# Six of seventeen gate tiles moved from the units of branch B to the following units of branch A

## The chip, the cores and the metric

The kernel runs on one core of one Trainium2 chip. It is one launch that takes all inputs from device memory and writes ten outputs there. The metric is the device time of an execution in microseconds; three runs of the kernel before gave a median of 2362.17 us (2360.77 to 2366.52).

## The reference

One layer of a streaming encoder, for a prompt of 2048 tokens and 8 running streams of 16 new tokens each, that have a cache of 512 positions. Model width is 1024.

```python
h = rms_norm(x, norm_g) * (1.0 + scale) + shift          # adaLN
qa, ka, va, za, qb, kb, vb, zb, ga, gb = split(h @ w_in)  # 4 x 512, 4 x 512, 2 x 1024
oa = diff_attention(rope(qa), rope(ka), va, lam)          # 4 heads, two softmaxes each, 64-token chunk mask
ob = stick_breaking_attention(qb, kb, vb)                 # 8 heads, strictly causal
ya = (rms_norm(oa, subln_g) * (1.0 - lam_init) * silu(za)) @ w_branch_a
yb = (ob * silu(zb)) @ w_branch_b
x = x + gate * ((sigmoid(ga) * ya + sigmoid(gb) * yb) @ w_out)
y = rms_norm(x, final_g)
```

The rotated keys and the values of both branches are outputs too. The part that matters here is the projection of the merge gates `ga` and `gb`: the last 2048 columns of `h @ w_in`. They are needed only in the last stage of the kernel, so it is open when they are computed.

## The kernel before

Tokens lie in 17 tiles of 128 rows: the prompt's tiles 0 to 15, and a tile called `NT` (16) with the 8 x 16 sample tokens. Single-precision products are made of three half-precision ones (high by high, high by low, low by high), so every projection of a tile with inner dimension 1024 is 3 x 8 = 24 matmuls of up to 512 columns.

*Stages.* A first stage makes the normed and modulated `h`, splits it in two half-precision parts and stores it transposed (`hT_d`). The middle stage, which takes most of the time, runs through 8 units. The last stage merges the branches, does the attention of the sample tokens over their caches, and makes the final norm.

*Units.* Unit `u` has head group `u // 2` of branch `u % 2`: even units are branch A (differential attention, one head), odd units branch B (stick breaking, two heads). A unit passes over its tiles in the order NT, 0, 1, ... 15. For each tile it projects query, key, value and the silu gate (one `project`, 12 pieces of 2 matmuls), transposes query and key on TensorE (`transpose_qk`, beside piece 5 of the next projection), and for the prompt's tiles computes scores against all earlier tiles (`scores`), turns them to weights, and multiplies by the values two tiles later (`PV_LAG`, `pv`). A prompt tile `t` costs about (t + 1) blocks, so tiles at the start of a unit are small and tiles at its end large.

*Branch A* evacuates scores on DVE (L546), takes exponentials on ACT (L119 from L580), combines both softmaxes on DVE (L591), splits on ACT and DVE, and transposes the weights by DMA (L568). *Branch B* takes two sigmoids of the scores on ACT (L119 from L550 and L551), scans on DVE (L604), multiplies on GpSimd (L610), splits on ACT and DVE (L560, L561) and transposes by DMA. Scores use three PSUM banks, projections two, value products two; one bank, `t`, serves the gates, the transposes of query and key and some sums.

*Gates.* The 2048 gate columns are cut in four pieces of 512 by the table `GATES` (L58): only odd units have one, as wide as the table says. In an odd unit every tile has 12 pieces more (`gate_piece`, L485 to L496): 24 matmuls of the same `h` tile with the gate weights `wg` (L492), an eviction on ACT with a scale (L495), and a store to `g_d` (L496). The 17 gate tiles of each of the four odd units make 68.

*Order.* `line` (L858 to L868) holds the pieces of all projections and gates of all units in order. For each attention tile `take` (L876) cuts off as many pieces as the weight of the tile says (`duration`, L886, with a lead of 5 tiles), and `interleave` (L91) mixes them with the tile's scores and value products. So small tiles get few pieces and large tiles many, and the projections of the first tiles of a unit stand beside the largest tiles of the unit before it. The recording layer then has a scheduler that may move an instruction within an engine's queue where dependences allow.

*Weights.* `prepare_unit` (L305) returns 9 pieces for a unit of branch A and 18 for one of branch B: loads of 4 buffers of projection weights with their sums of squares on ACT (L270), the scale, the split of each in two halves; and the same for 4 buffers of gate weights. It is called when the unit before starts (L1220) and its pieces are spread over some ten tiles by `W_READY` (L1224). Buffers come from the list `free` and go back when a unit starts: those of the unit before it (L843). In tiles with no such piece left, `spare` (L1228) puts loads and sums of squares for the last stage.

The lines below are the functions that the diff touches.

Of the kernel before, what the change touches and what calls it, by code (L numbers as in the profile page):

```python
# [20 lines left out]
AF = mybir.ActivationFunctionType  # L21
# [6 lines left out]
KT = D // P  # L28
# [4 lines left out]
NT = SEQ // P  # L33
# [10 lines left out]
W_READY = 9  # L44
# [11 lines left out]
SAMPLE_TIME = 0.3  # L56

GATES = [(u // 2 * 512, u % 2 * 512) for u in range(8)]  # L58

C_ROPE = 0  # L60
C_ID = C_ROPE + 17 * 96
# [48 lines left out]
def layer_kernel(ctx: ExitStack, tc: tile.TileContext, a: dict):  # L110
    nc = tc.nc
    V, S, G, T = nc.vector, nc.scalar, nc.gpsimd, nc.tensor
# [61 lines left out]
    def buffers_of_4k(name, n):  # L174
        pool = ctx.enter_context(tc.tile_pool(name=name, bufs=1, side="right", reuse_waits="tile"))
        return [pool.tile([P, 1024], F32, name=f"{name}{i}") for i in range(n)]


    free = buffers_of_4k("wa", 8)
# [5 lines left out]
    def bank(tag, dt=F32):  # L185
        return ps.tile([P, 512 if dt == F32 else 1024], dt, tag=tag, name=f"ps_{tag}", bufs=BANKS[tag])
# [19 lines left out]
    def total(col, n=1):  # L206

        p = bank("t")
        T.matmul(p[:, 0:n], ones, col, start=True, stop=True)
        return p[:, 0:n]  # L210
# [54 lines left out]
    def sum_squares(src, n, dst, width=1024, scale=1.0):  # L265

        for i in range(0, n, width):
            junk = tiny.tile([P, width], F16, tag="junk", name="junk", bufs=1)
            w = min(width, n - i)
            S.activation(out=junk[:, 0:w], in_=src[:, i : i + w], func=AF.Square, scale=scale,  # L270
                         accum_out=dst[:, i // width : i // width + 1])

    def add_up(acc, n):
        if n == 1:
            return acc[:, 0:1]
        col = tiny.tile([P, 1], F32, tag="col", name="col")
        V.tensor_reduce(out=col, in_=acc[:, 0:n], axis=AX.X, op=ALU.add)
        return col
# [6 lines left out]
    def split(hi, lo, src, s, on=None):  # L285

        if on is S:
            S.activation(out=hi, in_=src, func=AF.Identity, scale=s)
        elif on is G:
            G.tensor_scalar(out=hi, in0=src, scalar1=s, scalar2=0.0, op0=ALU.mult, op1=ALU.add)  # L290
        else:
            V.tensor_scalar(out=hi, in0=src, scalar1=s, scalar2=None, op0=ALU.mult)
        V.scalar_tensor_tensor(out=lo, in0=src, scalar=s, in1=hi, op0=ALU.mult, op1=ALU.subtract)
# [8 lines left out]
    sh_box = []  # L302
    units = [None] * 8

    def prepare_unit(u, keep=None):  # L305


        h, kind = u // 2, u % 2
        U = dict(h=h, kind=kind, u=u, w=[], wg=[], bufs=[])
        units[u] = U  # L310
        raw = {}
        g0, gw = GATES[u]
        gk = 1024 // gw if gw else 0

        def fetch(name, k):
            raw[name, k] = b = free.pop(0) if keep is None else keep[:, k // 2, :]
            if name == "w":
                st = b.rearrange("p (k j n) -> p k j n", k=2, n=P)
                for i in range(2):
                    load(out=st[:, i, :, :], in_=w_in[:, k + i, :].rearrange("p (j n) -> p j n", n=512)[:, 4 * kind : 4 * kind + 4, h * P : (h + 1) * P])  # L320
            else:
                load(out=b.rearrange("p (k n) -> p k n", k=gk), in_=w_in[:, k : k + gk, 4096 + g0 : 4096 + g0 + gw])

        def norm(name, k, i):
            if k == 0:
                U[name + "acc"] = unit.tile([P, 4], F32, tag=name + "acc", name=name + "acc")
            fetch(name, k)
            sum_squares(raw[name, k], 1024, U[name + "acc"][:, i : i + 1])

        def bounds():  # L330
            fsq = total(add_up(U["wacc"], 4))
            U["sw"] = scales(fsq, unit, "sw")
            U["fsq"] = unit.tile([P, 1], F32, tag="fsq", name="fsq")
            V.tensor_copy(out=U["fsq"], in_=fsq)

        def bounds_g():
            U["sg"] = scales(total(add_up(U["gacc"], KT // gk)), unit, "sg")

        def split_to(name, k):

            b = free.pop(0)
            U["bufs"].append(b)
            if keep is None:
                free.append(raw[name, k])
            return raw[name, k], b.bitcast(F16)

        def cut(k):
            st, w = split_to("w", k)
            for i in range(2):
                x = w.rearrange("p (i f n) -> p i f n", i=2, f=2)[:, i, :, :]  # L350
                split(x[:, 0, :], x[:, 1, :], st[:, i * 512 : (i + 1) * 512], U["sw"][:, 0:1], S if i % 2 else G)
                U["w"].append(x)

        def gate_cut(k):
            st, w = split_to("g", k)
            w = w.rearrange("p (k f n) -> p k f n", k=gk, f=2)
            split(w[:, :, 0, :], w[:, :, 1, :], st.rearrange("p (k n) -> p k n", k=gk), U["sg"][:, 0:1], S if k else G)
            U["wg"].append(w)

        pieces = [lambda k=k: norm("w", k, k // 2) for k in range(0, KT, 2)] + [bounds] + [lambda k=k: cut(k) for k in range(0, KT, 2)]  # L360
        if gw:
            pieces += [lambda k=k: norm("g", k, k // gk) for k in range(0, KT, gk)] + [bounds_g] + [lambda k=k: gate_cut(k) for k in range(0, KT, gk)]
        return pieces
# [40 lines left out]
    def project(U, t):  # L404

        kind, h, sc, sq = U["kind"], U["h"], U["sc"], U["sq"]
        g, i = t // 4, t % 4
        box = {}
# [70 lines left out]
                load(out=s_d[U["u"]][:, 6:8, :], in_=vt.rearrange("p c f d -> p c (f d)"))  # L479
            U["q16", t], U["k16", t] = qb, k16  # L480

        g0, gw = GATES[U["u"]]
        per = 1024 // gw if gw else 0

        def gate_piece(n):  # L485

            if n == 0:
                box["g"] = bank("t")
            for j in range(per * n, per * n + per):
                hi, wi = ((0, 0), (0, 1), (1, 0))[j % 3]  # L490
                k = j // 3
                T.matmul(box["g"][:, 0:gw], box["h"][:, hi, k, :], U["wg"][k // per][:, k % per, wi, :], start=(j == 0), stop=(j == 3 * KT - 1))  # L492
            if per * n + per == 3 * KT:
                gt = gts[:, t % 2 * 512 : t % 2 * 512 + 512]
                S.activation(out=gt[:, 0:gw], in_=box["g"][:, 0:gw], func=AF.Identity, scale=sc[:, 6:7])  # L495
                load(out=g_d[t][:, g0 : g0 + gw], in_=gt[:, 0:gw])  # L496

        return [lambda n=n: piece(n) for n in range(12)] + [lambda n=n: gate_piece(n) for n in range(3 * KT // per if gw else 0)]
# [334 lines left out]
    back = []  # L833
# [6 lines left out]
    def begin(u, t):  # L840
        if t == NT:
            if u > 0:
                free.extend(units[u - 1]["bufs"])  # L843
            finish_unit(u)

    def projection(m):
        u, t = steps[m]
        made = []

        def piece(i):  # L850
            if i == 0:
                begin(u, t)
                made.extend(project(units[u], t))
            if i == H_AT and not at_hand and m + 1 < len(steps):
                fetch_h(*steps[m + 1])
            made[i]()

        return [lambda i=i: piece(i) for i in range(12 + 3 * GATES[u][1] // 128)]  # L858

    starts = []  # L860
    for m in range(len(steps)):
# [24 lines left out]
    def duration(t):  # L886
        return SAMPLE_TIME if t == NT else TILE_TIME + (t + 1) / 4
# [327 lines left out]
    for n in range(len(steps) + PV_LAG):  # L1215
        made, qk, vs = [], [], []
        if n < len(steps):
            u, t = steps[n]
            past += duration(t)
            if t == NT and u < 7:  # L1220
                back += prepare_unit(u + 1)
            if u == 7 and not back and not spare and len(branch_weights) > 1:
                branch_weight()
            if back:  # L1224
                for fn in back[: -(-len(back) // max(1, W_READY - t % NT))]:
                    back.pop(0)()
            else:
                for _ in spare[: -(-len(spare) // ((NT + 1 - t % NT) + 8 * (6 - min(u, 6))))]:  # L1228
                    spare.pop(0)()
            if t < NT:  # L1230
                qk = scores(units[u], t, made)
        if n >= PV_LAG:
            for job in jobs[n - PV_LAG]:
                vs += pv(job)
        target = position(len(steps) * past / whole + LEAD)
        pieces = take(target, min(n + 1, len(steps) - 1))
        if at[0] == len(line) and not pieces and not spare:
            if cuts is None:
                cuts = early_work()
            pieces = [(1.0, fn) for fn in cuts[: -(-len(cuts) // (len(steps) + PV_LAG - n))]]  # L1240
            del cuts[: len(pieces)]
        interleave(pieces, qk, (vs, V_LO, V_HI))
        jobs.append(made)
# [149 lines left out]
```

## Time and profile before

| | |
|---|---|
| median of three runs | 2362.17 us (2360.77 to 2366.52) |
| the profiled execution | 2363.25 us |
| its span, first to last instruction | 2361.2 us |
| mean granted TensorE clock | 0.960 |
| DVE busy | 73% of the span |
| ACT busy | 68% |
| DMA, mean of 16 engines | 77.4% (hardware queue) |

The page gives times of one profiled execution. PE is TensorE's matmuls, PEld its weight loads, DVE VectorE, ACT ScalarE, POOL GpSimd, SP the queue that issues DMAs. A line such as L492 is a line of the kernel before. In rows of groups stand the busy time in microseconds, the mean of one in nanoseconds, and the idle time just ahead of them with what ended it. In rows of waits stand the waiting instruction, what released it, the total in microseconds, the number of times, and the longest.

### The profile page before, as it was taken

What the parts mean: (1) busy time and instruction counts of PE and PEld (TensorE: products, weight loads), DVE (VectorE), ACT (ScalarE), POOL (GpSimd) and SP (SyncE); (2) the same over time, 40 slices, a digit from 0 to 9 for tenths busy, and PEclk for the clock granted to TensorE, in tenths of its full rate; (3) what the DMA queues carried; (4) which work ended last, traced back from release to release, by engine and by line L of the source; (5) the groups of instructions that cost most, each with busy time, mean ns of one, the idle gap of its engine ahead of it and who ended that gap; (6) DMA issues with size and microseconds to landing.
All of it is one profiled execution on the core that took longest, in us unless ns stands there. A gap on an engine that the chain in (4) does not pass through costs nothing. (4 is left out here: it accounts for less than half of the span.)

```text
span 2361.2 us, 42524 instructions
## 1 busy us (share of the span) xinstructions
PE 2122.7 (90%) x15272; PEld 1147.9 (49%) x15272; DVE 1734.8 (73%) x3604; ACT 1602.7 (68%) x3116; POOL 724.7 (31%) x595
## 2 busy tenths in 40 slices
PE   3979899998999899799999989999995788889998
PEld 1645554445555445445554544554543344444553
DVE  3868756779775667977667797777778877888764
ACT  3658777777786777878677787866777555555641
POOL 0633002346410233631023364103334332233221
PEclk7989999999999999999999999999996899999999
DMA  9657859987796888878688797866687999999531
GB/s 321 243 169 201 218 133 234 206 199 162 188 236 135 196 198 184 179 174 193 147 197 181 179 184 180 196 149 155 150 178 170 281 250 252 257 233 255 168 100 54
DMA packets 843571, 453.73 MB, mean 192 GB/s; under 512 B 538234, under 2 KB 786346, under 8 KB 842848
## 3 DMA queue, kind: packets, MB, share of 16 engines
q1 hardware_dynamic: 843360, 451.03, 77.4%
q8 instruction: 119, 1.95, 0.4%
q14 instruction: 92, 0.75, 0.1%
HBM read 249.80 MB, written 73.44 MB: 137 GB/s over the span
## 5 line engine op out<-in xcount | busy, mean ns | idle before, releaser
L610 POOL TENSOR_TENSOR sc_p<-sc_p,sc_n 128x127 f32<-128x127 f32 (+7 forms) x192 | 307.5, 1606 | 896.5 <-DVE sc_n L604 885.6
L425 PE MATMUL ps_mm<-wb,hs 128*128 128x512 f16 x1632 | 414.1, 381 | 1.3 <-DMA hs<-hT_d 1.1
L425 PEld LDWEIGHTS <-hs 128*128 128x128 f16 x3120 | 272.1, 99 | 257.1 <-DMA hs<-hT_d 17.1
L425 PE MATMUL ps_mm<-wa,hs 128*128 128x512 f16 x1488 | 373.6, 383 | 14.2 <-DMA hs<-hT_d 12.0
L604 DVE TENSOR_TENSOR_SCAN sc_n<-ps_s,sc_n,zero_t 128x512 f32<-128x512 f32 x192 | 245.4, 1278 | 75.6 <-ACT ps_s L119 72.2
L561 DVE TENSOR_TENSOR sc_n<-sc_p,sc_n 128x128 f16<-128x128 f32 (+7 forms) x192 | 222.2, 1161 | 50.1 <-ACT sc_n L560 49.6
L627 PE MATMUL ps_s<-k,qst 128*128 128x512 f16 (+3 forms) x640 | 226.5, 355 | 34.8 <-DVE sc_n L604 31.7
L492 PEld LDWEIGHTS <-hs 128*128 128x128 f16 x1632 | 155.9, 98 | 184.0 <-DVE qst L520 6.9
L119 ACT ACTIVATE sc_p<-ps_s,usc 128x512 f32<-128x512 f32 (+3 forms) x320 | 203.2, 635 | 41.0 <-PE ps_s L628 27.1
L628 PE MATMUL ps_s<-k,qst 128*128 128x512 f16 (+3 forms) x640 | 226.8, 355 | 0.0
L679 PE MATMUL ps_o<-v,wt 128*128 128x128 f16 x1088 | 175.1, 227 | 34.8 <-DMA wt<-sc_n 34.6
L560 ACT CAST sc_n<-sc_p 128x128 f16<-128x128 f32 (+7 forms) x192 | 154.5, 806 | 72.9 <-POOL sc_p L610 72.3
L119 ACT ACTIVATE ps_s<-ps_s,usc 128x512 f32<-128x512 f32 (+3 forms) x328 | 198.2, 604 | 0.0
L492 PE MATMUL ps_t<-wa,hs 128*128 128x512 f16 x816 | 193.8, 382 | 3.2 <-DVE qst L520 3.2
L492 PE MATMUL ps_t<-wb,hs 128*128 128x512 f16 x816 | 189.0, 379 | 3.0 <-DVE qst L520 2.9
L1310 PE MATMUL ps_o<-wo,wa 128*128 128x512 f16 x816 | 186.2, 383 | 0.7 <-ACT wa L1134 0.7
L680 PE MATMUL ps_o<-v,wt 128*128 128x64 f16 x1088 | 160.6, 199 | 0.0
L679 PEld LDWEIGHTS <-wt 128*128 128x128 f16 x1088 | 107.0, 102 | 102.4 <-DMA wt<-sc_n 47.0
L546 DVE TENSOR_SCALAR_CACHE_REDUCE sc_p<-ps_s,usc 128x512 f32<-128x512 f32 (+3 forms) x160 | 106.3, 664 | 47.2 <-PE ps_s L628 27.6
L546 DVE TENSOR_SCALAR_CACHE_REDUCE sc_n<-ps_s,usc 128x512 f32<-128x512 f32 (+3 forms) x160 | 106.3, 665 | 46.1 <-PE ps_s L628 27.2
L604 DVE TENSOR_TENSOR_SCAN sc_n<-ps_s,zero_t 128x128 f32<-128x128 f32 (+3 forms) x128 | 104.3, 815 | 48.4 <-ACT ps_s L119 47.0
L680 PEld LDWEIGHTS <-wt 128*128 128x128 f16 x1088 | 104.5, 101 | 56.4 <-issue 2.5
(341 smaller groups left out, 4495.9 us busy)
## 6 DMA issues: line engine op xcount, KB each, us to landing
hs<-hT_d SPq DMA_DIRECT2D x130, 512.0 KB, 4.5
g_d<-gt SPq DMA_DIRECT2D x68, 256.0 KB, 4.3
wb<-g_d SPq DMA_DIRECT2D x34, 512.0 KB, 5.1
out_dram<-pr SPq DMA_DIRECT2D x204, 64.0 KB, 2.1
z_d<-pr SPq DMA_DIRECT2D x136, 64.0 KB, 2.3
o_d<-o SPq DMA_DIRECT2D x136, 64.0 KB, 2.2
hs<-z_d SPq DMA_DIRECT2D x17, 512.0 KB, 5.8
hs<-o_d SPq DMA_DIRECT2D x17, 512.0 KB, 4.3
```

What stands on the lines that cost most here:

```text
L119: i = S.activation(**kw)
L425: T.matmul(box["p"], box["h"][:, hi, k, :], U["w"][k][:, wi, :], start=(n == 0), stop=(n == 3 * KT - 1))
L492: T.matmul(box["g"][:, 0:gw], box["h"][:, hi, k, :], U["wg"][k // per][:, k % per, wi, :], start=(j == 0), stop=(j == 3 * KT - 1))
L546: V.tensor_scalar(out=dst[:, lo : lo + n], in0=p[:, 0:n], scalar1=sc_pos, scalar2=None, op0=ALU.mult, op1=ALU.max, accum_out=job["mx"][:, ...
L561: V.tensor_tensor(out=lo, in0=src, in1=hi, op=ALU.subtract)
L604: V.tensor_tensor_scan(out=dst[:, lo : lo + n][:, ::-1], data0=src[:, 0:n][:, ::-1], data1=zero_t[:, 0:1].to_broadcast([P, n]), initial=fi ...
L610: G.tensor_tensor(out=p[:, 0:m], in0=p[:, 0:m], in1=n[:, 1 : m + 1], op=ALU.mult)
L627: T.matmul(p[:, 0:n], qst[:, c, :], kk[:, c, 0:n], start=True, stop=False)
L628: T.matmul(p[:, 0:n], qst[:, 2 + c, :], kk[:, c, 0:n], start=False, stop=not diag)
L679: T.matmul(po[:, c * P : (c + 1) * P], wt[:, wj, :], vt[:, c, :, :], start=first, stop=False)
L680: T.matmul(po[:, c * P : c * P + 64], wt[:, nb + wj, :], vt[:, c, 0, :], start=False, stop=last)
L1310: T.matmul(po, st["y"][:, yi * 8 + k, :], wo[j * 4 + k // 2][:, wi, k % 2, :], start=(n == 0), stop=(n == 3 * KT - 1))
```

## The change

The gate tiles NT, 0, 1, 2, 3 and 4 of units 1, 3 and 5 are projected by units 2, 4 and 6, in the step of the same token tile, with the same `h` tile that this step has loaded for its own projection. Tiles 5 to 15 stay, and unit 7 keeps all of its 17. So units 1, 3 and 5 now have 11 steps of 24 pieces and 6 of 12, and units 2, 4 and 6 have 6 of 24 and 11 of 12. The gate weights' buffers of a B unit are given back after tile 4 of the A unit, not at its start. For this the weights of the unit after it are prepared from tile 3 of the A unit on, not from its first tile, spread as if two more tiles were to be had, and the spare work is held back in tiles NT, 0, 1 and 2 of units 2, 4 and 6. No instruction is added or removed.

```diff
+GATES_LATER = [NT, 0, 1, 2, 3, 4]
...
+    def gates_of(u, t):
+        if u % 2 == 0:
+            return u - 1 if u > 0 and t in GATES_LATER else None
+        return None if u < 7 and t in GATES_LATER else u
...
-        g0, gw = GATES[U["u"]]
+        ug = gates_of(U["u"], t)
+        g0, gw = GATES[ug] if ug is not None else (0, 0)
...
-                T.matmul(box["g"][:, 0:gw], box["h"][:, hi, k, :], U["wg"][k // per][:, k % per, wi, :], start=(j == 0), stop=(j == 3 * KT - 1))
+                T.matmul(box["g"][:, 0:gw], box["h"][:, hi, k, :], units[ug]["wg"][k // per][:, k % per, wi, :], start=(j == 0), stop=(j == 3 * KT - 1))
...
-                S.activation(out=gt[:, 0:gw], in_=box["g"][:, 0:gw], func=AF.Identity, scale=sc[:, 6:7])
+                S.activation(out=gt[:, 0:gw], in_=box["g"][:, 0:gw], func=AF.Identity, scale=units[ug]["sc"][:, 6:7])
+                if ug < U["u"] and t == GATES_LATER[-1]:
+                    free.extend(units[ug]["bufs"][4:])
...
-                free.extend(units[u - 1]["bufs"])
+                free.extend(units[u - 1]["bufs"][0:4])
...
-        return [lambda i=i: piece(i) for i in range(12 + 3 * GATES[u][1] // 128)]
+        return [lambda i=i: piece(i) for i in range(12 if gates_of(u, t) is None else 24)]
...
-            if t == NT and u < 7:
+            if t == (3 if u % 2 == 0 and u > 0 else NT) and u < 7:
                 back += prepare_unit(u + 1)
...
-                for fn in back[: -(-len(back) // max(1, W_READY - t % NT))]:
+                for fn in back[: -(-len(back) // max(1, W_READY + (2 if u % 2 == 0 and u > 0 else 0) - t % NT))]:
                     back.pop(0)()
-            else:
+            elif u % 2 or u == 0 or t not in (NT, 0, 1, 2):
                 for _ in spare[: -(-len(spare) // ((NT + 1 - t % NT) + 8 * (6 - min(u, 6))))]:
                     spare.pop(0)()
```

## The prediction, made before the changed kernel ran

> **What bounds the kernel now.** I read the page's first part, then a table of stretches, then waits, in that order.
>
> ```profile
> span 2361.2 us, 42524 instructions
> ...
> PE 2122.7 (90%) x15272; PEld 1147.9 (49%) x15272; DVE 1734.8 (73%) x3604; ACT 1602.7 (68%) x3116; POOL 724.7 (31%) x595
> ...
> L631 PE MATMUL ps_s<-masks,idb 128*128 128x64 bf16 (+1 forms) x256 | 53.0, 207 | 0.0
> ```
>
> TensorE is busy 90% of the span. All matmuls stay, so the change can only win or lose TensorE idle time, and an average doesn't say where that lies. The 256 mask matmuls (L631) are two for each of 16 token tiles in 8 units; their starts date the tiles. I cut the affected transitions by them: tile 12 of an A unit to tile 4 of the next B unit ("A ends": units 0, 2, 4), tile 12 of a B unit to tile 3 of the next A unit ("B ends": units 1, 3, 5), and the A middles (tiles 3 to 12). Columns of this table: length, then busy us of PE, PEld, DVE, ACT, POOL, then clock and DMA share.
>
> ```profile
> 259.00:355.00 96.00, 92.60 (x667) 52.99 (x666) 60.60 (x146) 67.23 (x139) 5.22 (x8) 0.98 0.66 153
> 688.00:778.00 90.00, 88.95 (x638) 49.39 (x636) 55.03 (x136) 62.94 (x132) 5.28 (x8) 1.00 0.70 158
> 1114.00:1199.00 85.00, 85.00 (x613) 47.64 (x612) 56.83 (x138) 59.48 (x125) 6.26 (x8) 1.00 0.62 145
> 485.00:582.00 97.00, 87.11 (x680) 48.73 (x679) 84.85 (x115) 78.53 (x150) 55.48 (x39) 0.96 0.87 187
> 908.00:1008.00 100.00, 87.32 (x711) 48.81 (x709) 88.27 (x127) 78.12 (x150) 57.67 (x41) 1.00 0.89 187
> 1322.00:1423.00 101.00, 89.12 (x712) 49.23 (x711) 88.99 (x128) 78.75 (x152) 57.28 (x40) 0.98 0.86 185
> 582.00:688.00 106.00, 99.09 (x683) 53.88 (x682) 86.60 (x243) 86.74 (x206) 32.41 (x34) 0.98 0.83 204
> 1008.00:1114.00 106.00, 101.11 (x688) 54.56 (x686) 81.61 (x233) 83.57 (x197) 30.69 (x33) 0.98 0.77 187
> 1423.00:1527.00 104.00, 99.00 (x677) 53.38 (x676) 82.77 (x235) 83.45 (x196) 31.25 (x34) 1.00 0.75 190
> 1625.00:1734.00 109.00, 108.95 (x722) 56.53 (x720) 75.75 (x114) 77.56 (x147) 35.85 (x23) 1.00 0.66 149
> ```
>
> The A ends (rows 1 to 3) are TensorE alone: idle 3.4, 1.1 and 0 us, DVE and ACT at 61 to 70%. The B ends (rows 4 to 6) aren't: TensorE idles 9.9, 12.7 and 11.9 us, DVE works 87 to 88%. What TensorE waits for there, in the last three tiles of unit 3:
>
> ```profile
> PE ps_s L627 <- DVE sc_n L604: 6.4, 7, 2.0
> ```
>
> The scan (L604) must finish before its score bank is free. So the change takes work from a place where TensorE sets the time and puts it where it has some room: 34.5 us of idle in the three B ends together. The question is whether that room holds what arrives.
>
> **The change, part by part.** *What moves.* A gate tile is 24 matmuls of 512 columns. Their pace:
>
> ```profile
> 689.78 4.26 PE L492 MATMUL ps_t<-wb,hs 128*128 128x512 f16 x19
> 693.88 0.38 PE L627 MATMUL ps_s<-k,qst 128*128 128x512 f16 x1
> 694.09 0.38 PE L628 MATMUL ps_s<-k,qst 128*128 128x512 f16 x1
> ```
>
> 19 take 4.26 us of which the last's 0.38 overlaps nothing: (4.26 - 0.38) / 18 = 0.216 us each, 5.2 us a tile. Counted between mask matmuls in the order of the built programs, the A ends lose 144, 144 and 125 gate matmuls, the B ends gain 144 each and lose 10, 17 and 17 projection matmuls, which come back in the next stretches.
>
> *B ends, longer.* 134, 127 and 127 matmuls by 0.216 are 28.9, 27.4 and 27.4: 83.7 us. Filling every idle microsecond leaves 83.7 - 34.5 = 49.2 us more. A saturated stretch does fill: the last row of the table, a B middle, shows 108.95 busy of 109. Busy time overstates a lone matmul (0.38 counted, 0.216 needed), so there is rather more room than 34.5; I take 2 us more a stretch, less 1 us for the small A tiles that stay unfilled: **+46**. Bounds: +36 (4.4 us more room a stretch) and +66 (half the idle stays).
>
> What else arrives there:
>
> ```profile
> L495 ACT ACTIVATE gt<-ps_t,usc 128x512 f32<-128x512 f32 x6 | 4.1, 685 | 11.5 <-PE ps_t L492 11.5
> L270 ACT ACTIVATE junk<-wa 128x1024 f16<-128x1024 f32 x6 | 6.3, 1055 | 0.2
> ...
> L288 ACT ACTIVATE v<-ps_mm,usc 128x128 f16<-128x128 f32 x6 | 2.2, 361 | 0.0
> L293 DVE SCALAR_TENSOR_TENSOR v<-ps_mm,usc,v 128x128 f16<-128x128 f32 x6 | 2.1, 345 | 0.3 <-ACT v L288 0.3
> ```
>
> ```profile
> PE ps_t L492 <- DVE qst L520: 6.1, 3, 3.2
> ```
>
> ```profile
> SPq L496 <- ACT gt L495: 34.8, 34, 4.4
> ```
>
> Six evictions of 0.685 us join ACT: 78 + 4 in a stretch that becomes some 115 us, so they hide behind TensorE. The gate bank is the single one that the query and key transposes use; in A units ACT, not DVE, copies these out, and a gate that comes too early holds up TensorE, with scores and value products behind it (whole run: 3 waits, the longest 3.2 us). The six gate stores go through SP, which waits about 1 us for an eviction (34.8 / 34), with the weight transposes (L568) behind. I cost both at nothing, since TensorE as the bound gives the transposes time; without that cover about 1 us a tile, 18 in all, which lies within the upper bound.
>
> *A ends, shorter.* TensorE keeps 92.6 - 31.1 = 61.5, 89.0 - 31.1 = 57.9 and 85 - 27 = 58 us. ACT loses six evictions (4.1) and, since the preparation of the unit after next starts later, two squares (2.1), and gains two to four splits (0.36 each, so 1): 62, 58 and 54. DVE stays at 61, gets 57 in unit 2 (six splits of 0.35 come earlier) and stays at 57. Nothing is above 62 and three engines are level, so dependences decide. The nearest rows with all three loaded are the A middles: their DVE and ACT work 77 to 82%. At 0.80 the busier of DVE and ACT gives 62 / 0.80 = 77.5, 72 and 71 us. To that I add 2.5 us each for this wait, seen where the tiles of unit 0 ran fast (244 to 281 us):
>
> ```profile
> PE ps_o L675 <- DMA wt<-sc_n: 6.3, 2, 3.4
> ```
>
> The value products come two tiles after the softmax; shorter tiles leave its transposes less time, and a wait blocks TensorE's queue. So 80, 74.5 and 73.5 against 96, 90 and 85: 16 + 15.5 + 11.5 = **-43**. Bounds: at 0.88, the DVE share of the B ends, without waits 70.5, 65.5 and 64.5, -70; at 0.72, about the ACT share of the A ends today, 86, 80 and 79, -26.
>
> *What comes back.* The 44 projection matmuls that the B ends lose (9.5 us) take the place of 19 gate matmuls that have left there; some 26 matmuls, 6 us, land in A middles and in unit 7, where TensorE is 93 to 100% busy: **+6**. The preparation of units 3 and 5 starts four tiles later and finishes two later: four squares of 1.055 us go from the B ends to each A middle, where ACT (79 to 82%) has cover from TensorE. Weights are ready some three tiles before their first use, so no wait; if either fails, 6 us more. If the middles absorb all, 0.
>
> Sum: -43 + 46 + 6 = +9 us. On the profiled execution, 2363.25 us (span 2361.2 and 2 us around it), 2372; that execution is 1.1 us above the median of 2362.17, so against the median I say **2371**.
>
> *A rule that speaks against the change.* With few matmuls the clock falls:
>
> ```profile
> 139.00:160.00 21.00, 10.51 (x52) 4.75 (x51) 13.57 (x38) 7.85 (x22) 5.45 (x6) 0.67 0.78 280
> ...
> 1734.00:1805.00 71.00, 54.04 (x426) 31.03 (x423) 61.84 (x74) 55.09 (x95) 33.46 (x17) 0.81 0.80 166
> ```
>
> The first tiles of unit 0 have hardly a projection beside them: clock 0.67. In the new order the first two tiles of units 1, 3 and 5 have neither projection nor gate. [...]
>
> **The rivals.**
> - *Faster.* The A ends run DVE and ACT at the 0.88 of the B ends: -70 + 46 + 6 = -18, 2344. For it: their wait rows are short, and at 688 to 778 TensorE waited 1 us. Against: no A stretch shows over 0.82, and the transposes wait where tiles are fast.
> - *No change.* 0.80 without transpose waits, -50.5: +1.5, 2364. For it: idle time is only shuffled. Against: 83.7 us arrive where 34.5 are free.
> - *Slower, the transposes.* A ends stay at 0.72 because value products block TensorE: -26 + 46 + 6 = +26, 2388. It decides when two tiles pass in less than the softmax, splits and transposes need.
> - *Slower, the clock.* As in unit 0, 21 x (1 - 0.67) / 0.5 = 14 us at half rate in each start of units 1, 3 and 5; about 16 us of matmuls (48 projections, value products) then take up to 14 more, half of it hidden by ACT: 3 x 7 = 21 on top of +9, 2392.
> - *It doesn't do what it says.* The scheduler could have put other work in the gaps; the built order shows the gates where the change puts them, so I give it nothing.
>
> **How the numbers follow.** Forecast 0.42 (its own range 2364 to 2380), faster 0.27, no change 0.18, transposes 0.08, clock 0.05. A measurement here can tell 0.3%, about 7 us, from no change. Faster takes its rival and 0.02 of the no-change case: 0.29. Same takes 0.16 of that and the forecast's lower end, 0.10: 0.26. The rest, 0.45, is slower. The range takes in the faster case and both slow ones: 2343 to 2394; the extremes of all bounds (2328 and 2414) need everything to go one way.
>
> **What would show it.** Right: B ends of 113 to 117 us with TensorE over 97% busy and no scan wait; A ends of 73 to 80 us with TensorE at 75 to 80% and all else as before; the middles 0 to 3 us longer. Wrong: A ends below 70 us (faster rival), value products waiting over 4 us per A end (transposes), a clock under 0.9 there (clock), or B ends under 110 us, which would mean that busy time hid more room than I grant.

## The result, and the profile after

The changed kernel takes 2376.33 us (median of 7 runs, 2371.58 to 2381.41), the kernel before in the same session 2365.39 (7 runs, 2360.77 to 2368.47). The ratio is 1.0056, 95% interval 1.0039 to 1.0072: slower by 13 us (9 to 17). The forecast of +9 is close, in sign and size. Its terms are not all right, and that they cancelled is in part luck; the experiments below show which ones did.

Lines of the changed kernel are 8 to 11 higher than before: L425 is L433, L492 is L501, L604 is L615, L627 is L638, L675 is L686, L568 is L579. First the head of its page.

```profile
span 2370.5 us, 42541 instructions
...
PE 2129.2 (90%) x15272; PEld 1150.4 (49%) x15272; DVE 1716.2 (72%) x3604; ACT 1601.8 (68%) x3116; POOL 708.3 (30%) x595
```

As many matmuls as before and 9.3 us more span; TensorE's busy time grows by 6.5 us. (The page counts 17 instructions more. They are semaphore instructions; the counts of the engines' work are those of before.) The work is the same, so where each microsecond went must be read by stretches. This is the table of stretches of the changed kernel, with the columns of the prediction's table: A ends of units 0, 2, 4 (three rows), B ends of units 1, 3, 5 (three), A middles of units 2 and 4 (two), and, new here, the B middles (tile 4 to tile 12 of units 1, 3, 5) and the first tile of each B middle (tile 4 to tile 5).

```profile
256.00:331.00 75.00, 65.34 (x518) 39.20 (x516) 57.30 (x141) 58.78 (x124) 6.04 (x7) 0.95 0.76 163
687.00:752.00 65.00, 59.66 (x470) 34.41 (x468) 53.75 (x137) 55.10 (x117) 3.96 (x6) 1.00 0.66 152
1108.00:1176.00 68.00, 60.40 (x477) 35.70 (x475) 53.00 (x133) 52.84 (x113) 4.15 (x6) 0.97 0.70 148
465.00:578.00 113.00, 112.58 (x849) 61.18 (x846) 79.39 (x120) 81.80 (x154) 45.94 (x35) 1.00 0.87 189
888.00:1002.00 114.00, 112.41 (x844) 60.98 (x843) 78.86 (x121) 80.71 (x155) 46.81 (x35) 1.00 0.85 180
1313.00:1427.00 114.00, 111.74 (x834) 60.39 (x833) 77.45 (x119) 80.31 (x154) 46.81 (x35) 1.00 0.81 177
578.00:687.00 109.00, 99.83 (x681) 54.60 (x679) 83.60 (x232) 84.48 (x199) 31.16 (x38) 0.99 0.83 203
1002.00:1108.00 106.00, 100.60 (x688) 55.07 (x687) 84.14 (x234) 84.85 (x199) 31.13 (x38) 0.98 0.82 198
331.00:465.00 134.00, 121.70 (x771) 61.57 (x769) 94.80 (x153) 101.59 (x200) 42.52 (x29) 0.96 0.86 195
752.00:888.00 136.00, 122.11 (x782) 62.12 (x780) 91.09 (x152) 100.95 (x198) 41.85 (x30) 0.96 0.82 195
1176.00:1313.00 137.00, 122.81 (x785) 62.63 (x783) 92.14 (x155) 95.09 (x185) 42.12 (x30) 0.94 0.71 170
331.00:366.00 35.00, 26.36 (x153) 12.59 (x151) 21.70 (x49) 21.84 (x47) 8.91 (x8) 0.90 0.80 194
752.00:779.00 27.00, 21.35 (x146) 11.21 (x144) 21.73 (x51) 18.45 (x41) 9.68 (x9) 0.94 0.77 184
1176.00:1215.00 39.00, 28.18 (x155) 13.45 (x153) 23.70 (x52) 22.05 (x47) 8.79 (x9) 0.79 0.71 175
```

The same view of the kernel before, for the B middles and their first tiles, which the prediction did not show:

```profile
355.00:485.00 130.00, 120.07 (x770) 61.03 (x769) 91.33 (x148) 97.85 (x190) 39.79 (x28) 0.99 0.90 214
778.00:908.00 130.00, 120.24 (x777) 61.12 (x776) 87.49 (x147) 95.82 (x186) 39.56 (x28) 0.99 0.83 194
1199.00:1322.00 123.00, 117.64 (x766) 60.23 (x764) 87.12 (x144) 92.19 (x177) 39.49 (x28) 0.99 0.82 191
355.00:377.00 22.00, 18.81 (x111) 9.21 (x110) 17.42 (x41) 15.58 (x33) 8.90 (x7) 0.92 0.76 195
778.00:798.00 20.00, 18.09 (x117) 9.11 (x116) 16.70 (x40) 12.29 (x27) 6.79 (x7) 1.00 0.72 169
1199.00:1222.00 23.00, 20.81 (x122) 10.11 (x120) 16.42 (x43) 16.23 (x34) 6.49 (x7) 0.93 0.80 198
```

The reader is to see four things. The B ends are as forecast: 112.58 of 113 us busy, clock 1.00. The A ends are shorter than forecast: 75, 65 and 68 us, not 80, 74.5 and 73.5. The B middles, which had no term, are longer. And that growth lies in the one tile right behind an A end: 35, 27 and 39 us for 22, 20 and 23, with a clock of 0.90, 0.94 and 0.79. That is 36 us more in these three tiles, while the whole B middles grow by 24: the tiles behind them got shorter. Half of the 36 is busy time (75.9 us for 57.7), since by the counts in brackets the three tiles hold 42, 29 and 33 matmuls more, some of them at the lower clock; the other half, 17.8 us, is idle time of TensorE.

What TensorE waited for, in the whole run of the changed kernel (first two rows), in the A ends (next three), in the B ends (next three, the only rows there), and in the first tiles of the B middles of units 1 and 5:

```profile
PE ps_mm L433 <- DMA hs<-hT_d: 29.2, 8, 8.4
PE ps_s L638 <- DVE sc_n L615: 12.6, 12, 1.9
...
PE ps_o L686 <- DMA wt<-sc_n: 6.6, 5, 2.5
PE ps_o L686 <- DMA wt<-sc_n: 1.3, 2, 0.8
PE ps_o L686 <- DMA wt<-sc_n: 6.8, 4, 2.9
...
PE ps_o L690 <- DMA wt<-sc_n: 0.4, 1, 0.4
PE ps_o L690 <- DMA wt<-sc_n: 1.6, 1, 1.6
PE ps_o L690 <- DMA wt<-sc_n: 2.3, 1, 2.3
...
PE ps_mm L433 <- DMA hs<-hT_d: 6.3, 1, 6.3
PE ps_mm L433 <- DMA hs<-hT_d: 7.5, 1, 7.5
```

The wait for the scan fell from 31.7 us (row below) to 12.6: the B ends no longer wait for it. The wait for a tile of `h` grew from 13.1 us to 29.2. These are the two rows of before:

```profile
PE ps_s L627 <- DVE sc_n L604: 31.7, 37, 2.0
PE ps_mm L425 <- DMA hs<-hT_d: 13.1, 5, 8.4
```

What was issued before that tile shows in the queue SP of the changed kernel ahead of the wait in unit 1 (start, length, instruction):

```profile
320.73 12.87 SPq L579 DMA_TRANSPOSE wt<-sc_n  x7
...
348.87 0.34 SPq L838 DMA_DIRECT2D wa<-in_w_out_dram  x1
349.31 0.38 SPq L410 DMA_DIRECT2D hs<-hT_d  x1
```

Seven transposes held the queue for 12.87 us, others follow, and the fetch of `h` goes out at 349.31, behind them and a spare load that itself waited 2.2 us for a buffer. In the first tile of unit 3 TensorE shows no wait for `h`; its longest there, 2.8 us, is for transposed weights. (A wait of 3.2 us for `h` comes later in the same B middle.) In windows of 2 us the clock around the other two waits is this. In unit 1 TensorE has no matmul from 347.9 to 354.2 us, and the clock reads 1.00 to 351, 0.96 to 353, 0.50 in the three windows to 359, 0.84 in the next, and 1.00 from 361. In unit 5 it has none from 1196.5 to 1203.9, and the clock reads 1.00 to 1198, then 0.83, 0.50 in four windows, 0.61, and 1.00 from 1210. But unit 5's tile begins at 0.50 too, from 1176 to 1182, ahead of that wait. The reading to be tested is that the short tiles of an A end use up `h` faster than this queue, with three buffers, brings it.

### The profile page after: what moved, and what is told of

Same layout as the page of the kernel before. It is cut to its first block, busy times and chain, and to the rows that moved or that the text cites. A ratio compares the mean times of both kernels' runs of the same rounds, so it can differ in the third digit from the quotient of the medians.

```text
span 2370.5 us, 42541 instructions
## 1 busy us (share of the span) xinstructions
PE 2129.2 (90%) x15272; PEld 1150.4 (49%) x15272; DVE 1716.2 (72%) x3604; ACT 1601.8 (68%) x3116; POOL 708.3 (30%) x595
## 5 line engine op out<-in xcount | busy, mean ns | idle before, releaser
L433 PEld LDWEIGHTS <-hs 128*128 128x128 f16 x3120 | 280.4, 99 | 302.8 <-DMA hs<-hT_d 31.7
L433 PE MATMUL ps_mm<-wa,hs 128*128 128x512 f16 x1590 | 394.5, 384 | 20.3 <-DMA hs<-hT_d 20.3
L433 PE MATMUL ps_mm<-wb,hs 128*128 128x512 f16 x1530 | 382.7, 383 | 9.0 <-DMA hs<-hT_d 8.9
L615 DVE TENSOR_TENSOR_SCAN sc_n<-ps_s,sc_n,zero_t 128x512 f32<-128x512 f32 x192 | 245.8, 1280 | 84.2 <-ACT ps_s L121 80.1
L638 PE MATMUL ps_s<-k,qst 128*128 128x512 f16 (+3 forms) x640 | 227.6, 356 | 22.0 <-DVE sc_n L615 12.6
L572 DVE TENSOR_TENSOR sc_n<-sc_p,sc_n 128x128 f16<-128x128 f32 (+7 forms) x192 | 199.9, 1048 | 59.5 <-ACT sc_n L571 58.7
L501 PEld LDWEIGHTS <-hs 128*128 128x128 f16 x1632 | 152.0, 98 | 173.9 <-DVE qst L531 8.9
L501 PE MATMUL ps_t<-wb,hs 128*128 128x512 f16 x816 | 195.4, 382 | 5.5 <-DVE qst L531 5.2
L690 PE MATMUL ps_o<-v,wt 128*128 128x128 f16 x1088 | 168.0, 226 | 32.4 <-DMA wt<-sc_n 30.9
L501 PE MATMUL ps_t<-wa,hs 128*128 128x512 f16 x816 | 194.6, 381 | 2.3 <-DVE qst L531 2.3
L1322 PE MATMUL ps_o<-wo,wb 128*128 128x512 f16 x816 | 188.5, 386 | 0.7 <-ACT wb L1145 0.7
L615 DVE TENSOR_TENSOR_SCAN sc_n<-ps_s,zero_t 128x128 f32<-128x128 f32 (+3 forms) x128 | 103.7, 814 | 80.1 <-ACT ps_s L121 69.9
L691 PE MATMUL ps_o<-v,wt 128*128 128x64 f16 x1088 | 154.0, 198 | 0.0
L690 PEld LDWEIGHTS <-wt 128*128 128x128 f16 x1088 | 105.6, 102 | 90.7 <-DMA wt<-sc_n 41.2
L466 POOL TENSOR_TENSOR rot<-pr,rope 128x256 f32<-128x256 f32 x68 | 54.4, 799 | 281.7 <-ACT pr L447 226.1
L686 PE MATMUL ps_o<-v,wt 128*128 128x128 f16 x544 | 103.0, 226 | 33.3 <-DMA wt<-sc_n 33.1
```

The lines of the kernel that those rows point to most:

```text
L433: T.matmul(box["p"], box["h"][:, hi, k, :], U["w"][k][:, wi, :], start=(n == 0), stop=(n == 3 * KT - 1))
L501: T.matmul(box["g"][:, 0:gw], box["h"][:, hi, k, :], units[ug]["wg"][k // per][:, k % per, wi, :], start=(j == 0), stop=(j == 3 * KT - 1))
L572: V.tensor_tensor(out=lo, in0=src, in1=hi, op=ALU.subtract)
L615: V.tensor_tensor_scan(out=dst[:, lo : lo + n][:, ::-1], data0=src[:, 0:n][:, ::-1], data1=zero_t[:, 0:1].to_broadcast([P, n]), initial=fi ...
L638: T.matmul(p[:, 0:n], qst[:, c, :], kk[:, c, 0:n], start=True, stop=False)
L690: T.matmul(po[:, c * P : (c + 1) * P], wt[:, wj, :], vt[:, c, :, :], start=first, stop=False)
```

## The experiments

All twelve runs are told here. Ratios are to the kernel before in the same session, with 95% intervals; microseconds are such a ratio times its median. The lengths below are worked out from the starts of the mask matmuls in each profiled execution and summed over the units (us; "last" is tile 12 of unit 6 to tile 12 of unit 7; "rest" is the span less the five columns). They show where the time went; the verdicts rest on the ratios. Each row is one execution, and its span can lie some us from the median (`prep_only` was profiled at 2380.99 us with a median of 2387.32, `later_3` at 2355.15 with 2347.97). The changed kernel and `after_h2`, which differ little, agree within 3.0 us in every column.

| kernel | A ends (0, 2, 4) | B middles (1, 3, 5) | B ends (1, 3, 5) | A middles (2, 4, 6) | last | rest | span |
|---|---|---|---|---|---|---|---|
| before | 270.7 | 383.1 | 298.6 | 316.0 | 206.9 | 885.9 | 2361.2 |
| changed | 207.9 | 407.0 | 340.6 | 319.6 | 214.6 | 880.8 | 2370.5 |
| `a_light` | 218.9 | 395.4 | 297.3 | 318.4 | 208.8 | 887.1 | 2325.9 |
| `b_heavy` | 274.0 | 391.3 | 341.0 | 312.4 | 217.1 | 880.4 | 2416.2 |
| `prep_only` | 282.3 | 384.1 | 279.9 | 336.5 | 214.5 | 881.6 | 2378.9 |
| `six_early` | 213.4 | 395.1 | 350.1 | 306.6 | 211.3 | 878.2 | 2354.7 |
| `after_h4` | 209.7 | 387.6 | 341.7 | 318.5 | 213.4 | 886.4 | 2357.3 |
| `before_h4` | 272.1 | 375.9 | 306.9 | 312.7 | 206.3 | 877.0 | 2350.9 |
| `later_3` | 240.0 | 394.0 | 304.9 | 321.7 | 209.6 | 883.1 | 2353.3 |
| `later_last3` | 244.1 | 404.5 | 318.7 | 312.0 | 211.5 | 878.9 | 2369.7 |
| `three_early` | 242.2 | 389.0 | 315.4 | 304.4 | 210.6 | 886.0 | 2347.6 |

### Does the late `h` tile give the gain back? A first try

Changed kernel and kernel before, each with `h` fetched two steps ahead instead of one, in the same three buffers:

```diff
-            if i == H_AT and not at_hand and m + 1 < len(steps):
-                fetch_h(*steps[m + 1])
+            if i == H_AT and not at_hand:
+                for s in steps[m + 1 : m + 3]:
+                    if s not in ahead and s not in sent:
+                        sent.add(s)
+                        fetch_h(*s)
```

> The changed kernel, but each h tile is fetched two steps ahead of its projection, not one (three buffers hold them). In the changed kernel's profile the A ends gave 63 us, the B ends took 42, and the next stretch of units 1, 3 and 5 (tiles 4 to 12) took 24 more that the prediction did not have; projections there wait for an h tile (6.3, 3.2 and 7.5 us in one wait each in units 1, 3 and 5), since a step without gates leaves it half the lead in SP's queue. Theory 1, the late h tile is what gives the gain back: these waits go, with the half clock that follows them, and the time falls by 14 to 24 us to 2352 to 2362. Theory 2, the tail of branch A's last softmax and the transposes in SP's queue set the pace there and the h tile is only the last to come: the time stays within 5 us of 2376.

> The kernel before with the same fetch two steps ahead, as the control. Both theories: it has only some 6 us of such waits in the middle units (1.0, 0.8, 2.2, 1.8, 1.1), so the time falls by 0 to 6 us, to 2359 to 2365. If it falls by as much as the changed kernel, the earlier fetch is a gain of its own and says nothing about the change.

Changed: 1.0027 (1.0011 to 1.0044). Before: 0.9988 (0.9977 to 1.0000). The waits for `h` behind the A ends stayed at 6.4 and 5.6 us. The fetch behind the first A end still goes out in the same place of the queue, behind the seven transposes and the same spare load (at 350.46 us, for 349.31). The likely reason, argued and not tested alone, is that with three buffers a tile can't be fetched before one is free. The expected gain did not come, and the try did not do what it was to test.

### The arrivals: the six gate tiles made twice

The changed kernel, but units 1, 3 and 5 also keep their own six gate tiles. So the A ends are full as before, and what is added is the work in the B ends together with the later preparation of weights:

```diff
-        return None if u < 7 and t in GATES_LATER else u
+        return u
```

> The A units project the six tiles' gates as in the changed kernel, and the B units go on projecting all their gates too, so these 18 gate tiles are made twice: the price of the arrivals alone, with A ends as before. Theory of the prediction, room of 34.5 us or a little more in the B ends: 18 x 5.2 = 93 us of matmuls cost 42 to 48, 2406 to 2413. Rival, the room is larger than busy time shows and half of them are hidden with the A starts: 2390 or less. Rival, no room, TensorE's queue makes all else wait: 2450.

1.0207 (1.0187 to 1.0226): +49 us. The B ends grow by 42.4 (341.0 for 298.6), as in the changed kernel; the rest comes in the B middles (+8.2), the A ends (+3.3) and the last stretch (+10.2), less 3.6 in the A middles. That is a little more than the 42 to 48 expected, and it is near the forecast's +46 and +6 together, though all 432 gate matmuls (93 us) are added here. But two edits are in it, which the later runs take apart.

### The departures: the gates lightened in place

The kernel before, with 2 of the 24 matmuls left in each of the six gate tiles of units 1, 3 and 5. 396 of 432 matmuls are gone, evictions and stores stay:

```diff
+    def thin(u, t):
+        return u in (1, 3, 5) and t in (NT, 0, 1, 2, 3, 4)
...
-        return [lambda i=i: piece(i) for i in range(12 + 3 * GATES[u][1] // 128)]
+        return [lambda i=i: piece(i) for i in range(13 if thin(u, t) else 12 + 3 * GATES[u][1] // 128)]
```

> The kernel before with 2 of 24 matmuls left in each of the six gate tiles of units 1, 3 and 5; eviction and store stay. The gates of these tiles are so left incomplete, and 18 x 22 x 0.216 = 86 us of matmuls are gone. It shows what the departure alone is worth. Theory 1 (A ends shrink till DVE, ACT and transposes level with TensorE, and the stretch after them gives part back): -30 to -43, 2322 to 2335. Rival, TensorE alone sets the time in these stretches: -75 to -86, 2279 to 2290.

0.9837 (0.9821 to 0.9853): -39 us (-35 to -42), inside the expected -30 to -43. With the 36 matmuls that stay (36 x 0.216 = 8 us at most) the full departure is worth -39 to -46. The A ends of this kernel, in the table of stretches:

```profile
257.00:338.00 81.00, 68.32 (x526) 41.61 (x525) 57.38 (x147) 61.18 (x131) 4.00 (x6) 0.92 0.83 181
688.00:760.00 72.00, 62.91 (x485) 35.95 (x484) 55.40 (x131) 59.03 (x128) 8.15 (x9) 0.98 0.75 175
1107.00:1173.00 66.00, 58.57 (x465) 33.38 (x464) 52.08 (x123) 56.44 (x122) 12.19 (x13) 1.00 0.69 155
```

They fall by 51.8 us in all (270.7 to 218.9), and 12.3 of it comes back in the B middles behind them, though nothing was added anywhere. So shortening A ends by itself lengthens what follows them. The late `h` tile is there too: TensorE waits for it 6.2, 6.5 and 3.0 us in the tiles behind the three A ends.

### Which tiles: three of the six

```diff
-GATES_LATER = [NT, 0, 1, 2, 3, 4]
+GATES_LATER = [NT, 0, 1]
```

and, in the second kernel, `[2, 3, 4]`.

> The changed kernel with only the first three tiles (NT, 0, 1) moved. The two halves of the change were measured alone: arrivals of six tiles a unit cost 49 us, departures give 38. Theory of the room: the B ends have 10 to 15 us of idle TensorE each and three tiles bring 15.6, so arrivals cost 3 to 15 us in all, while the first three to leave come out of a stretch where TensorE is never idle and give most of their 46.7 us, 28 to 40: 2328 to 2354, faster than both kernels. Rival, both halves are linear in the number of tiles: +5, about 2371.

> Instead the last three tiles (2, 3, 4) moved; NT, 0 and 1 stay with branch B. The same number of matmuls leaves and arrives, but these gates stood at the very end of the A end and beside the first small tiles of branch B. Theory of the room alone, the number counts and not which: as later_3 within 5 us. Rival, small tiles need work beside them (else TensorE falls to half clock and the softmax tail is bare): at least 10 us slower than later_3, 2350 to 2375.

With NT, 0 and 1: 0.9927 (0.9911 to 0.9942), faster than before, as expected. With 2, 3 and 4: 1.0034 (1.0018 to 1.0050), the time that its rival gave; the half clock that the rival named does not show in the mean clock, 0.958 for 0.957 of the first kernel. As many matmuls move in both, and 25 us lie between them. In the profiled executions it is 16.4 us, since the first kernel's was its slowest run. By the table 13.8 are in the B ends (318.7 for 304.9), 10.5 in the B middles and 4.1 in the A ends; the A middles of the second are 9.7 shorter. So room in the B ends is not a matter of how many gate matmuls arrive alone: where in the unit they stand matters too. (One thing more differs: the gate weights' buffers come free after tile 1 in the first kernel and after tile 4 in the second. No run separates the two.) Between them, three tiles of the one kind win 17 us, three of the other lose 8.

### The preparation alone

The kernel before with nothing moved but the preparation of weights and the spare work, by the three lines of the change that do this:

```diff
-            if t == NT and u < 7:
+            if t == (3 if u % 2 == 0 and u > 0 else NT) and u < 7:
...
-                for fn in back[: -(-len(back) // max(1, W_READY - t % NT))]:
+                for fn in back[: -(-len(back) // max(1, W_READY + (2 if u % 2 == 0 and u > 0 else 0) - t % NT))]:
...
-            else:
+            elif u % 2 or u == 0 or t not in (NT, 0, 1, 2):
```

> The kernel before with only the schedule of the change: weights of units 3 and 5 (and 7) prepared from tile 3 of the A unit on and the spare work held back in its first four tiles; no gate moves. As the prediction costed it: nothing, within 4 us of the kernel before. Rival, part of the loss is the later preparation: +5 or more.

1.0094 (1.0079 to 1.0109): +22 us. The expected 0 was wrong. Its B ends and the A middles of units 2, 4 and 6, in the table of stretches:

```profile
483.00:576.00 93.00, 82.18 (x672) 46.08 (x670) 83.87 (x117) 73.92 (x142) 51.87 (x35) 1.00 0.93 193
910.00:1003.00 93.00, 82.21 (x674) 46.15 (x672) 83.33 (x118) 73.53 (x142) 51.87 (x35) 1.00 0.90 193
1332.00:1425.00 93.00, 84.01 (x678) 46.85 (x676) 83.27 (x119) 73.48 (x142) 51.90 (x35) 0.98 0.88 194
576.00:689.00 113.00, 101.73 (x704) 55.37 (x703) 84.97 (x235) 86.17 (x204) 33.74 (x38) 0.98 0.76 184
1003.00:1114.00 111.00, 101.97 (x698) 55.73 (x697) 84.66 (x236) 87.15 (x205) 33.76 (x38) 0.98 0.75 180
1425.00:1538.00 113.00, 103.08 (x697) 56.47 (x696) 84.78 (x238) 86.86 (x205) 33.76 (x38) 0.96 0.75 176
```

In the profiled execution, which is 17.7 us longer than that of before, the B ends win 18.7 us, the A middles lose 20.5, the A ends 11.6 and the last stretch 7.6. In the A middles no engine is near its limit (TensorE 90 to 92%, ACT 76 to 79%), and ACT's busy time there is 0.6 us under to 3.6 over that of before: with so much idle time left, the squares by themselves don't explain it. What waits are the value products for transposed weights (26.0 us in the three A middles, 11.6 before), and in the queue SP the fetch of `h` for its buffer (first A middle):

```profile
PE ps_o L675 <- DMA wt<-sc_n: 10.2, 5, 3.6
SPq L402 <- PE ps_mm L425: 10.1, 5, 4.6
```

The same two rows of the kernel before, in its first A middle:

```profile
PE ps_o L675 <- DMA wt<-sc_n: 4.2, 4, 2.9
SPq L402 <- PE ps_mm L425: 2.7, 2, 2.2
```

Both waits have grown together, on one queue. That the one causes the other (a fetch that waits holds back the transposes behind it) fits the rows, but no run separates them. Nor does a run tell the later start of the preparation from the spare work held back: all three lines are in this one edit.

### The `h` tile again, now with a buffer for it

Changed kernel and kernel before, each with a fourth buffer for `h` and the fetch two steps ahead. Room for it comes from one buffer of projection staging and one value tile:

```diff
-V_BUFS = 23
+V_BUFS = 22
...
-        ahead[u, t] = hs[len(fetched) % 3].bitcast(F16).rearrange("p (f k n) -> p f k n", f=2, n=P)
+        ahead[u, t] = (hs + [h4])[len(fetched) % 4].bitcast(F16).rearrange("p (f k n) -> p f k n", f=2, n=P)
...
-            pr = stg.tile([P, 512], F32, tag="pr", name="pr", bufs=3)
+            pr = stg.tile([P, 512], F32, tag="pr", name="pr", bufs=2)
```

> The run with the fetch two steps ahead left the order of the DMA queue almost as it was, and so tested nothing: with three buffers an h tile cannot go out earlier. Here the changed kernel has a fourth h buffer (the staging tiles of projections go from 3 to 2 and the value tiles from 23 to 22 to make room) and the fetch two steps ahead. Theory 1, the late h tile: its waits of 6 to 8 us in units 1 and 5 go and the half clock after them, 8 to 20 us less, 2355 to 2368. Theory 2, the tail of branch A and the transposes in the queue: within 5 us of 2376, with TensorE waiting for something else in the same place.

> Control for the fourth buffer: the kernel before with it, the fetch two steps ahead, and the smaller staging. Theory 1: it has only 4.7 us of waits for h tiles in the middle stage to lose, 0 to 6 us less, 2359 to 2365. If it gains as much as the changed kernel did (17 us), the fourth buffer says nothing about the change.

Changed: 0.9967 (0.9955 to 0.9980), 21 us off its 1.0056. Before: 0.9955 (0.9941 to 0.9968), 11 us. The second missed its expectation of 0 to 6 us. The wait for `h` in the whole run of the changed kernel with four buffers, TensorE's longest wait in the first tile of its B middle in unit 1, and the first tiles of its B middles:

```profile
PE ps_mm L433 <- DMA hs<-hT_d: 9.1, 1, 9.1
...
PE ps_t L516 <- ACT gt L504: 3.7, 1, 3.7
...
335.00:366.00 31.00, 26.55 (x164) 13.29 (x163) 20.48 (x49) 20.72 (x47) 7.84 (x7) 0.89 0.84 211
747.00:775.00 28.00, 24.64 (x171) 12.69 (x169) 21.96 (x53) 20.09 (x46) 9.28 (x9) 1.00 0.72 169
1169.00:1200.00 31.00, 24.60 (x175) 13.01 (x173) 22.27 (x54) 20.60 (x45) 11.14 (x9) 1.00 0.81 183
```

The one wait left is in the first tiles of unit 0, where the changed kernel and the kernel before have one of 8.4. The clock in unit 5 is 1.00 where it was 0.79; in unit 1 it stays at 0.89, where a wait of 3.7 us for a gate's eviction has taken the place of the one for `h`. The B middles go from 407.0 to 387.6 us, while the A ends stay short (209.7). But half of the gain is to be had without the change too, so only some 10 us of it belong to the change. The same holds for the stretch: in the control the edit takes 7.1 us from the B middles (383.1 to 375.9), where the waits for `h` had been 4.7 us in all, apart from the one of 8.4 in unit 0. So the late tile explains some 12 of the 23.9 us by which the B middles grew; with four buffers they are still 11.7 us longer than the control's.

### The six tiles with the preparation of before

The changed kernel with the three lines of the preparation put back:

```diff
-            if t == (3 if u % 2 == 0 and u > 0 else NT) and u < 7:
+            if t == NT and u < 7:
...
-                for fn in back[: -(-len(back) // max(1, W_READY + (2 if u % 2 == 0 and u > 0 else 0) - t % NT))]:
+                for fn in back[: -(-len(back) // max(1, W_READY - t % NT))]:
...
-            elif u % 2 or u == 0 or t not in (NT, 0, 1, 2):
+            else:
```

> The changed kernel (six tiles moved), but with the schedule of the kernel before: weights of the next unit prepared from the A unit's first tile on, spare work not held back. Theory 3, the late preparation is a third part of the change that costs about 22 us by itself wherever it stands (departure -38, arrivals about +27, preparation +22): 2350 to 2360, faster than the kernel before. Rival, in the run of the preparation alone it cost because branch B's first gates came up before their weights, and with these gates moved it costs nothing: 2370 to 2380.

0.9958 (0.9944 to 0.9972): 10 us faster than before, where the changed kernel is 13 us slower. The moved gates are a gain; the later preparation turns it into a loss. That also speaks against the rival of this run, that the preparation alone had cost time only because branch B's first gates came before their weights: it gave 2370 to 2380 us, and 2352.61 were measured. Its first B end and its A middles of units 2 and 4:

```profile
465.00:583.00 118.00, 114.58 (x845) 61.72 (x843) 84.77 (x132) 86.33 (x164) 49.18 (x39) 0.99 0.79 176
583.00:688.00 105.00, 98.54 (x675) 53.53 (x673) 80.68 (x229) 85.36 (x196) 28.38 (x34) 1.00 0.90 221
1006.00:1107.00 101.00, 97.66 (x683) 53.40 (x682) 79.66 (x224) 81.93 (x193) 29.50 (x34) 1.00 0.85 214
```

Against the changed kernel its B ends are 9.5 us longer in sum, its A middles 13.0 shorter and its B middles 11.9 shorter. Its waits for `h` are nearly those of the changed kernel (28.2 us for 29.2), so this part of the B middles' growth comes with the later preparation and not with a late tile.

### Three tiles, early preparation, four buffers

`GATES_LATER = [NT, 0, 1]` with the lines of the last run, and the same with the fourth `h` buffer:

> Three tiles moved (NT, 0, 1) and the early preparation. Theory 3: later_3 (2348) less 10 to 22: 2326 to 2338. Rival as above: 2343 to 2353.

> As three_early, with the fourth h buffer and the fetch two steps ahead. Theory 1: the remaining waits for h tiles (10.7 us in the run of three tiles) go: 5 to 12 us less than three_early. Rival: its smaller staging costs as much as it brings, within 4 us.

0.9925 (0.9909 to 0.9942) and 0.9916 (0.9902 to 0.9929). The first missed its expectation: early preparation wins nothing over the 0.9927 of the three tiles with the late one. In the table the pattern is the one of six tiles (B ends 10.5 us longer, A middles 17.3 shorter, B middles 5.0 shorter, A ends 2.2 longer), and yet the medians don't differ. The second, 2343.61 us, is the fastest complete kernel of the study, 20 us under the kernel before, but only 3 us under the first, where 5 to 12 were expected; their intervals overlap.

## Why the prediction was right, and where it was not

**The sum.** +9 was forecast and +13 measured (9 to 17). By the table the profiled execution's +9.3 is made of -62.8 in the A ends, +23.9 in the B middles, +42.0 in the B ends, +3.6 in the A middles, +7.7 in the last stretch and -5.1 in the rest; the forecast was -43, +46 and +6. That the numbers meet is in good part luck, as the terms show.

**What moves: TensorE idle time.** Right. Both sides of the exchange were named: A ends bound by TensorE, B ends with too little room.

**A ends, -43.** Near the net worth, -39 to -46 by the lightened gates, but not for the reason given. The forecast was of the stretch, and the stretch lost 62.8 us (270.7 to 207.9), near the bound of -70: DVE and ACT work there 78 and 85 and 78% (58.78 of 75, 55.10 of 65, 53.00 of 68), about the 0.80 assumed, but they have less to do than the 62, 58 and 57 us put in. The transposes did hold up value products, 6.6, 1.3 and 6.8 us, above the mark of 4 in two of three, without deciding. Then 23.9 us came back in the B middles. This place was named nowhere: the prediction asked what DVE and ACT allow in shorter tiles, not how fast the queue brings `h` to them. Some 12 of those 23.9 go with the fourth buffer, as shown above, and 11.9 with the preparation of before; whether these two add up was not run.

**B ends, +46.** The stretch is right: +42.0, TensorE 98% busy or more in each, no scan wait. As a net worth it is too large. Taken alone with the preparation of before, the arrivals cost about 28 us by two differences, neither a run of its own: -10 for the six tiles less -39 for their departure is +29, and +49 for the gates made twice less +22 for the preparation is +27. With the 8 us that the lightened gates left in place, the first could be up to 37. Against it stand +46 and +6. The +6 is itself 5.4 by its own counts (44 less 19 matmuls are 25); A middles and last stretch grew by 11.3, but `prep_only`, which moves no gate, has the last stretch 7.6 longer too.

**The preparation later, at nothing: the step that failed.** The prediction put it so: the squares go to A middles "where ACT (79 to 82%) has cover from TensorE", weights are ready in time, "if either fails, 6 us more". Alone it costs 22 us, and between the six tiles with and without it lie 23. ACT's cover was not the point: its busy time there grew by 3.6 us at most, about the four squares that were counted, and other engines had room. The waits for transposes and for `h` buffers in the A middles grew. The 18 pieces that moved have loads and splits in them, and the argument counted the squares alone; which of them makes the waits stays open.

So -39, +28 and +22 stand for -43, +46 + 6 and 0: they sum to +11, near the +13 measured. The forecast's error on the arrivals hid its error on the preparation: that is the luck. That these pieces add up is itself not general: with three tiles the late preparation costs nothing that could be measured (0.9927 against 0.9925). Why stays open.

**The rivals.** *Faster* had the A ends right (below 70 us in two of three) but not the total. *Slower, the clock* named a real thing at another place: the clock in the A ends stays at 0.95, 1.00 and 0.97, and falls in the tile after them, to 0.90, 0.94 and 0.79, where TensorE waits 6.3 us (unit 1) and 7.5 (unit 5) for `h`. The half rate put into that rival is in the traces: in the kernel before, the start of unit 0 reads 0.50 in every microsecond from 143 to 156 us, with no matmul from 145 to 152, and in the changed kernel units 1 and 5 read 0.50 from late in these waits until 359 and 1208 us. By the rival's reckoning the three tiles hold 7, 3 and 16 us at half rate (35 x 0.10, 27 x 0.06 and 39 x 0.21, over 0.5), where it put 14 each. That the clock falls with few matmuls rests on the prediction's two rows (0.67 and 0.81) and these; how much idle time it takes, and whether the waits alone brought it on, no run shows. With `h` in time, unit 5 shows 1.00 there; unit 1 shows 0.89, behind another wait of 3.7 us.

## What to carry to other kernels

A change that moves work usually moves a schedule with it; price each separately, with the DMAs it issues, and run each alone: here, with six tiles, the move won 10 us and its companion lost 23. A stretch that gets shorter asks more of every queue that feeds it, so ask at what pace each can bring it (here seven transposes held one for 12.87 us), and look for the lost gain in the stretch right behind. Test a fetch further ahead only together with the buffer it needs, and give the kernel before the same buffer, or its own gain is put down to the change.

## What the runs showed that was not expected

- Asking for `h` one step earlier changed next to nothing in the kernel before with three buffers (0.9988); with a fourth it gave 0.9955.
- Transposes hold the issuing queue long: seven took 12.87 us of it, 1.17 to 2.67 us each, against 0.38 for a plain load of 512 KB (L410, the median of 130). The load of `h` behind them came late, though it landed 4.9 us after its issue (median of the 130: 4.4).
- Two sets of three gate tiles with equal work differ by 25 us, by their place in the unit and by when their weights' buffers come free.
- In unit 5 the tile with the wait of 7.5 us took 39 us at clock 0.79, and 31 at clock 1.00 with the wait gone, though it then held 20 matmuls more.
- A tile behind a shortened stretch also takes up work: 104 matmuls more stand in the three first tiles of the B middles, and TensorE is busy 18 us longer there, beside the time that it waits.
